# Turning the attention probabilities in halves of 64 queries, with the two heads' score tiles joined

## The chip, the core and the metric
The kernel runs on one core of one Trainium2 chip. The metric is the device time of one execution in microseconds; three runs of the kernel before gave 2627.28, 2629.58 and 2632.4 us, a median of 2629.58.

## The reference
A decoder block on a sequence of 2048 positions of width 1024: modulation from a condition vector, a token mixer, and a feed-forward part with a depthwise convolution. The token mixer has two groups of heads, gated linear attention (4 heads, called GLA here) and 8 softmax heads of width 64. Each softmax head runs three causal dilated windows, (window, dilation) = (128, 1), (512, 4) and (2048, 16), and merges them by their softmax denominators. Cut to the part that the change touches:

```python
def dilated_branch(q, k, v, slopes, window, dilation):
    ...
    s = jnp.einsum('bdhnqe,bdhnke->bdhnqk', qb, kw).astype(jnp.float32) * (E ** -0.5)
    ...
    s = jnp.where(valid, s + alibi, -jnp.inf)
    m = jnp.max(s, axis=-1, keepdims=True)
    p = jnp.exp(s - m)
    den = jnp.sum(p, axis=-1, keepdims=True)
    o = jnp.einsum('bdhnqk,bdhnke->bdhnqe', p, vw.astype(jnp.float32)) / den
    lse = (m + jnp.log(den))[..., 0]
    ...

def dilated_attention_group(q, k, v):
    ...
    weights = jax.nn.softmax(jnp.stack(lses, axis=0), axis=0)
    return jnp.einsum('gbsh,gbshe->bshe', weights, jnp.stack(outs, axis=0))
```

All of it is float32.

## The kernel before
The sequence is worked through in four chunks of 512 positions. For each chunk there are the input projection (`proj`), the mixing (`mix`: two halves of `gla`, then four calls of `attn`, one for each pair of heads), the output projection (`outproj`) and the feed-forward part (`ffn`). The large matrix products split each float32 operand into two parts and issue three matmuls for each product (L292, L293, L294 in `mm3`, 512 columns each, into PSUM banks called `psg`). `beside` (and `along`) writes the mixing of chunk c interleaved with the large products of the chunk before and after, so that TensorE always has large matmuls to issue between the small ones of the mixing. In the end the order on each engine is made by the framework's scheduler, which is switched on with the tile context (`schedule_with_timeline_sim`), from the written order, the dependences and its own estimate of durations. Each engine then executes its list in order.

A call of `attn` for a pair of heads holds, for the three windows, the tiles `s16` (128 queries by 4 blocks of nk = 32(c+1) keys, one tile for each head), `s4` and `sn` (128 queries by 4 blocks of 256 keys, one tile for each head, from the pool entry `big`). `scores` computes the products for the two heads, one on the upper 64 rows of the array and one on the lower 64 (L759; L795 for s16), VectorE adds the bias (L765), ScalarE takes the exponential (L769), VectorE scales by the merge factors (L844 for s4, L855 for sn). L824 and L848 are small products that carry these factors between layouts. Then the probabilities have to stand with keys on the partitions. `turn` (L774) does that for a head at a time: four turns by TensorE (L779) of 128 queries by up to 128 keys into one bank called `psa` (four such banks exist), and one copy back over the same tile, by ScalarE (L171) or VectorE (L173) in alternation. s16 needs one such round, s4 and sn two each (z = P and z = 0; one in chunk 0 for s4). L876 and L881 multiply the turned tiles by the values, L896 turns the result back.

Other places that the change touches: in `gla`, `la` (log decays) takes a buffer of the entry `s16`, and `gv` and `rg` (values and gates) two buffers of `big`; at the start `th` (L308) and the loads of the modulation weights (`wada`, L1017) use `big`. `big` has four buffers of 1024 columns, `s16` two of 512. L617 are the small products of `gla`. Loads and stores named here are issued by SyncE; the weights of the large products (L220) by GpSimd.

## Time and profile before
| | |
|---|---|
| Median of three runs | 2629.58 us |
| Profiled execution | 2630.91 us, its span 2629.1 us |
| TensorE (PE) busy | 2575.6 us, 98% |
| VectorE (DVE) busy | 1923.6 us, 73% |
| ScalarE (ACT) busy | 1278.6 us, 49% |
| GpSimd (POOL) busy | 242.9 us, 9% |
| DMA | 405.10 MB, mean 154 GB/s |

A row of a timeline gives the start, the length, the engine, the line, the operation, the tiles written and read, the shapes and how many instructions were merged into it. The matmuls overlap in time: each is shown from its start until its result is out, so what one takes of TensorE is the distance between the ends of two that follow each other. A matmul of float32 operands shows as two instructions, one of the split operands or a turn as one. "128*128" is the shape of the weights in the array (rows by columns), the second shape that of the operand that streams through it.

### The profile page before, as it was taken

To read this page: it belongs to the slowest core of one execution; us is meant where nothing else is said; L and a number is where in the kernel's file an instruction comes from. 1 tells how busy PE (TensorE), PEld (TensorE's weight loads), DVE (VectorE), ACT (ScalarE), POOL (GpSimd) and SP (SyncE) were. 2 spreads that over 40 slices of the span, in tenths; PEclk is the share of its full clock that TensorE was granted. 3 is DMA by queue.
4 is the path that set the end of the run, shared out by engine and by line. 5 is a ranking of instruction groups with operands and counts; after the bars stand their busy time and mean duration, and the time that the engine had idled before them with its cause. 6 is when DMAs were issued, how large, how long until landed. Compare 5 with 4: busy or idle time off the path is not lost.

```text
span 2629.1 us, 46905 instructions
## 1 busy us (share of the span) xinstructions
PE 2575.6 (98%) x18152; PEld 2112.5 (80%) x18152; DVE 1923.6 (73%) x4124; ACT 1278.6 (49%) x2619; POOL 242.9 (9%) x460
## 2 busy tenths in 40 slices
PE   5999999999999999999999999999999999999999
PEld 3888888788788888888788888877888888788887
DVE  7578877757778777776887777678777775666665
ACT  4556556646555444553545444445455443433332
POOL 0111111101000000000000000000000000000100
PEclk8999999999999999999999999999999999999999
DMA  8766574755633443346434444643344435332222
GB/s 292 255 212 237 195 242 164 232 162 185 210 127 99 130 131 122 117 137 208 141 98 131 140 135 131 235 141 104 122 141 138 136 118 185 128 104 96 97 96 88
DMA packets 192640, 405.10 MB, mean 154 GB/s; under 512 B 19985, under 2 KB 70946, under 8 KB 191138
## 3 DMA queue, kind: packets, MB, share of 16 engines
q0 software_dynamic: 60992, 220.49, 25.6%
q1 hardware_dynamic: 131426, 181.62, 20.8%
q8 instruction: 143, 2.34, 0.4%
q14 instruction: 79, 0.65, 0.1%
HBM read 339.12 MB, written 62.91 MB: 153 GB/s over the span
## 4 chain that ended last, share of the span: by engine, by line
PE 90%; DMA 4%; DVE 3%; issue 1%; ACT 1%; SPq 1%; POOL 0%; DVEq 0%; ACTq 0%
PE psg L292 26%; PE psg L294 25%; PE psg L293 25%; PE psa L759 3%; PE psa L779 2%; PE psa L881 2%; PE psa L617 1%; PE psa L795 1%; DMA x<-x 1%; DMA wada<-in_w_ada_dram 1%; PE psa L876 1%; DVE wlo L227 1%; PE psa L687 1%; PE psa L688 1%; DMA sq<-y 1%
## 5 line engine op out<-in xcount | busy, mean ns | idle before, releaser
L292 PE MATMUL psg<-hhi,whi 128*128 128x512 f32 x1992 | 786.7, 397 | 12.0 <-ACT hhi L428 5.7
L293 PE MATMUL psg<-hlo,whi 128*128 128x512 f32 x1992 | 783.5, 393 | 2.6 <-DVE hlo L430 2.6
L294 PE MATMUL psg<-hhi,wlo 128*128 128x512 f32 x1992 | 782.7, 393 | 0.8 <-DVE wlo L227 0.8
L226 ACT CAST whi<-wraw 128x1024 fp32r<-128x1024 f32 (+1 forms) x391 | 410.4, 1050 | 508.0 <-PE psg L293 404.0
L227 DVE TENSOR_TENSOR wlo<-wraw,whi 128x1024 fp32r<-128x1024 f32 (+1 forms) x391 | 478.0, 1223 | 175.7 <-ACT whi L226 169.9
L292 PEld LDWEIGHTS psg<-hhi,whi 128*128 128x128 f32 x1992 | 375.8, 189 | 99.3 <-ACT hhi L428 8.0
L293 PEld LDWEIGHTS psg<-hlo,whi 128*128 128x128 f32 x1992 | 376.1, 189 | 81.8 <-DVE hlo L430 3.6
L294 PEld LDWEIGHTS psg<-hhi,wlo 128*128 128x128 f32 x1992 | 375.9, 189 | 81.1 <-issue 1.5
L292 PE MATMUL psg<-ghi,whi 128*128 128x512 f32 x744 | 294.2, 398 | 2.7 <-ACT ghi L923 2.5
L294 PE MATMUL psg<-ghi,wlo 128*128 128x512 f32 x744 | 292.8, 394 | 1.6 <-DVE wlo L227 1.6
L293 PE MATMUL psg<-glo,whi 128*128 128x512 f32 x744 | 293.4, 394 | 0.5 <-DVE glo L924 0.5
L998 DVE SCALAR_TENSOR_TENSOR x<-psg,mod,x 128x512 f32<-128x512 f32 x192 | 143.0, 748 | 129.8 <-PE psg L294 127.8
L220 POOL DMA_DIRECT2D wraw<-in_w_up_dram x176 | 93.3, 530 | 1075.6 <-DVE wlo L227 949.0
L292 PE MATMUL psg<-whi,hhi 128*128 128x512 f32 (+2 forms) x512 | 174.1, 345 | 2.6 <-ACT stg L514 1.1
L294 PE MATMUL psg<-whi,hlo 128*128 128x512 f32 (+2 forms) x512 | 174.1, 343 | 0.0
L293 PE MATMUL psg<-wlo,hhi 128*128 128x512 f32 (+2 forms) x512 | 173.5, 340 | 0.0
L292 PEld LDWEIGHTS psg<-ghi,whi 128*128 128x128 f32 x744 | 139.4, 188 | 37.0 <-issue 5.2
L294 PEld LDWEIGHTS psg<-ghi,wlo 128*128 128x128 f32 x744 | 140.3, 189 | 32.2 <-DVE wlo L227 2.0
L293 PEld LDWEIGHTS psg<-glo,whi 128*128 128x128 f32 x744 | 140.3, 189 | 29.5 <-issue 1.4
L769 ACT ACTIVATE big<-big,nm 128x256 f32<-128x256 f32 (+1 forms) x256 | 122.4, 480 | 34.9 <-DVE nm L784 34.7
L953 ACT ACTIVATE y<-psg,conv_b_sb,conv_w_sb 128x512 f32<-128x512 f32 x176 | 136.2, 776 | 3.4 <-PE psg L294 2.0
L954 DVE SCALAR_TENSOR_TENSOR y<-psg,conv_w_sb,y 128x511 f32<-128x511 f32 x176 | 130.7, 743 | 1.4 <-ACT y L953 1.3
(222 smaller groups left out, 3417.7 us busy)
## 6 DMA issues: line engine op xcount, KB each, us to landing
wraw<-in_w_up_dram POOLq DMA_DIRECT2D x176, 512.0 KB, 3.6
wraw<-in_w_down_dram POOLq DMA_DIRECT2D x88, 512.0 KB, 3.6
wraw<-in_w_ch_dram POOLq DMA_DIRECT2D x44, 512.0 KB, 4.2
v<-v SPq DMA_DIRECT2D x68, 256.0 KB, 5.5
wada<-in_w_ada_dram POOLq DMA_DIRECT2D x64, 256.0 KB, 4.8
wraw<-in_w_tokw_dram POOLq DMA_DIRECT2D x32, 512.0 KB, 4.1
wraw<-in_w_out_dram POOLq DMA_DIRECT2D x32, 512.0 KB, 4.4
sq<-in_xT_dram SPq DMA_DIRECT2D x48, 256.0 KB, 3.8
```

Source lines behind the costliest of these rows:

```text
L220: (nc.gpsimd if self.planned else nc.sync).dma_start(raw[:, :n], src)
L226: nc.scalar.copy(hi[:, :n], raw[:, :n])
L227: nc.vector.tensor_tensor(lo[:, :n], raw[:, :n], hi[:, :n].bitcast(F32), op=ALU.subtract)
L292: nc.tensor.matmul(ps, wh, hh, start=first and k == 0, stop=False, skip_group_check=shared)
L293: nc.tensor.matmul(ps, wh, hl, start=False, stop=False, skip_group_check=shared)
L294: self.lastmm = nc.tensor.matmul(ps, wl, hh, start=False, stop=k == n - 1, skip_group_check=shared)
L759: nc.tensor.matmul(at(i, hh, z), q[H[hh], i * P:(i + 1) * P], key(H[hh], i, z), start=True, stop=True, skip_group_check=True)
L769: nc.scalar.activation(t[:, lo:hi], t[:, lo:hi], AF.Exp, bias=nm[:, hh, g, i:i + 1], scale=2.0 ** -(h + 1), accum_out=dn[:, hh, g, i:i + 1])
L779: nc.tensor.transpose(ps[:n, i * P:(i + 1) * P], part(S[hh], i), self.C("id"))
L953: nc.scalar.activation(y, ps, AF.Identity, bias=self.cb[:, b:b + 1], scale=self.cw[:, 2, b:b + 1])
L954: nc.vector.scalar_tensor_tensor(y[:, 1:], ps[:, :T - 1], self.cw[:, 1, b:b + 1], y[:, 1:], op0=ALU.mult, op1=ALU.add)
L998: nc.vector.scalar_tensor_tensor(x1, ps, self.mod[:, 40 + cb:41 + cb], x1, op0=ALU.mult, op1=ALU.add)
```

## The change
`turn` now takes both heads at once. The tiles of a window are one tile for the two heads: `s16` [128, 2, 512], `s4` and `sn` [128, 2, 4, 256]. A round turns, for each block i and head, first the queries 0 to 63 (rows 0 to 63 of the array) into one bank and then the queries 64 to 127 (rows 64 to 127) into a second bank; each of these turns streams 64 columns where one streamed 128 before. One copy for each bank brings back the 64 queries of both heads. In chunk 0 the turns of sn leave out the same block as before. The pool entries follow: `big` has two buffers of 2048 columns, `s16` one of 1024; `gv` and `rg` are halves of one buffer, `th` takes `s16`, and `la` the first half of `s16`, of which there is now one.

```diff
-        th = self.at.tile([P, 1024], F32, name="big", bufs=4)
+        th = self.at.tile([P, 1024], F32, name="s16", bufs=1)
...
-        la = t2("s16", 2)
+        la = self.at.tile([P, 1024], F32, name="s16", bufs=1)[:, 0:T]
...
-        gv, rg = big(), big()
+        big = self.at.tile([P, 2048], F32, name="big", bufs=2)
+        gv, rg = big[:, 0:1024], big[:, 1024:2048]
...
-        s16 = [self.at.tile([P, T], F32, name="s16", bufs=2) for _ in range(2)]
+        s16 = self.at.tile([P, 2, T], F32, name="s16", bufs=1)
+        s16b = s16[:, :, 0:4 * nk].rearrange("p h (i n) -> p h i n", i=4)
...
         def turn(n, b0, part, to):
 
-            for hh in range(2):
-                ps = self.pa()
-                for i in range(b0, 4):
-                    nc.tensor.transpose(ps[:n, i * P:(i + 1) * P], part(S[hh], i), self.C("id"))
-                self.copy(to(S[hh]), ps[:n, b0 * P:].rearrange("p (r n) -> p r n", n=P))
+
+            ps = [self.pa(), self.pa()]
+            for i in range(b0, 4):
+                for hh in range(2):
+                    for m in range(2):
+                        B = slice(64 * m, 64 * m + 64)
+                        nc.tensor.transpose(ps[m][:n, (4 * hh + i) * 64:(4 * hh + i + 1) * 64], part[B, hh, i], self.C("id")[B, B])
+            for m in range(2):
+                self.copy(to[:n, :, b0:, 64 * m:64 * m + 64], ps[m][:n].rearrange("p (h i q) -> p h i q", h=2, i=4)[:, :, b0:])
...
-        s4 = [self.at.tile([P, 4, 256], F32, name="big", bufs=4) for _ in range(2)]
-        sn = [self.at.tile([P, 4, 256], F32, name="big", bufs=4) for _ in range(2)]
+        s4 = self.at.tile([P, 2, 4, 256], F32, name="big", bufs=2)
+        sn = self.at.tile([P, 2, 4, 256], F32, name="big", bufs=2)
...
-        turn(nk, 0, lambda t, i: t[0][:, i * nk:(i + 1) * nk], lambda t: t[0][:nk].rearrange("p (r n) -> p r n", n=P))
+        turn(nk, 0, s16b, s16.rearrange("p h (i q) -> p h i q", i=4))
...
-            turn(P, 0, lambda t, i: t[1][:, i, z:z + P], lambda t: t[1][:, :, z:z + P])
+            turn(P, 0, s4[:, :, :, z:z + P], s4[:, :, :, z:z + P])
...
-            b0 = 0 if (c or z) else 1
-            turn(P, b0, lambda t, i: t[2][:, i, z:z + P], lambda t: t[2][:, b0:, z:z + P])
+            turn(P, 0 if (c or z) else 1, sn[:, :, :, z:z + P], sn[:, :, :, z:z + P])
...
+        bigs = [self.at.tile([P, 2048], F32, name="wada", tag="big", bufs=2) for _ in range(2)]
         for k in range(KD):
-            big = [self.at.tile([P, 1024], F32, name="wada", tag="big", bufs=4)]
+            big = [bigs[k % 4 // 2][:, k % 2 * 1024:k % 2 * 1024 + 1024]]
```

All other reads and writes of these tiles are rewritten for the new shapes (`outs[hh][...]` becomes `outs[:, hh, ...]`, and so on). In the changed file the turns are line L783, L824 is L828, L848 is L852, L876 is L879.

The scheduler makes another order from this. TensorE, second chunk, second pair of heads: the beginning of the turns of s4 (`big`), behind the small product of the merge factors. Before:

```order
L848 MATMUL psa<-xm,consts_sb 128x32
L779 MATMUL psa<-consts_sb,big 128x128 x12
L292 MATMUL psg<-ghi,whi 128x512
L293 MATMUL psg<-glo,whi 128x512
L294 MATMUL psg<-ghi,wlo 128x512
```

Now, at the same place:

```order
L852 MATMUL psa<-xm,consts_sb 128x32
L783 MATMUL psa<-consts_sb,big 128x64 x3
L292 MATMUL psg<-ghi,whi 128x512
L783 MATMUL psa<-consts_sb,big 128x64 x29
L293 MATMUL psg<-glo,whi 128x512
L294 MATMUL psg<-ghi,wlo 128x512
```

The 16 turns of s4 stood as 12 and, ten large matmuls later, 4; the 32 half turns stand as 3 and 29 with one large matmul between. The turns of sn that follow in the same call, on TensorE, before:

```order
L293 MATMUL psg<-glo,whi 128x512
L779 MATMUL psa<-consts_sb,big 128x128 x5
L294 MATMUL psg<-ghi,wlo 128x512
L779 MATMUL psa<-consts_sb,big 128x128 x3
L292 MATMUL psg<-ghi,whi 128x512
L293 MATMUL psg<-glo,whi 128x512
L779 MATMUL psa<-consts_sb,big 128x128 x4
L294 MATMUL psg<-ghi,wlo 128x512
```

And now:

```order
L294 MATMUL psg<-ghi,wlo 128x512
L292 MATMUL psg<-ghi,whi 128x512
L783 MATMUL psa<-consts_sb,big 128x64 x32
L293 MATMUL psg<-glo,whi 128x512
L294 MATMUL psg<-ghi,wlo 128x512
```

These 16 turns stood in four runs (4, 5, 3, 4); the 32 halves stand in one, 18 large matmuls behind the run of 29. The end of the turns of s4 on TensorE in the same call (the run of 29 above), now, with the numbers of the banks; psa_10903 and psa_10904 are the banks of the first round, psa_10923 and psa_10924 those of the second, in each pair first the bank of queries 0 to 63:

```order
L783 MATMUL psa_10903<-consts_sb_452,big_10575 128x64
L783 MATMUL psa_10904<-consts_sb_452,big_10575 128x64
L783 MATMUL psa_10923<-consts_sb_452,big_10575 128x64 x4
L783 MATMUL psa_10924<-consts_sb_452,big_10575 128x64 x5
L783 MATMUL psa_10923<-consts_sb_452,big_10575 128x64
L783 MATMUL psa_10924<-consts_sb_452,big_10575 128x64
```

The two halves mostly alternate, but where a bank came free late in the scheduler's reckoning, several halves of one bank stand together. Over the whole program the 600 turns stood in 99 unbroken runs, the 1200 halves stand in 98.

## Rows read from the trace of the kernel before

**Rows 1.** The page: busy time, share and instructions of TensorE; the chain of waits that ended last, by engine and by line.

```profile
PE 2575.6 (98%) x18152; PEld 2112.5 (80%) x18152; DVE 1923.6 (73%) x4124; ACT 1278.6 (49%) x2619; POOL 242.9 (9%) x460
...
PE 90%; DMA 4%; DVE 3%; issue 1%; ACT 1%; SPq 1%; POOL 0%; DVEq 0%; ACTq 0%
PE psg L292 26%; PE psg L294 25%; PE psg L293 25%; PE psa L759 3%; PE psa L779 2%; PE psa L881 2%; PE psa L617 1%; PE psa L795 1%; DMA x<-x 1%; DMA wada<-in_w_ada_dram 1%; PE psa L876 1%; DVE wlo L227 1%; PE psa L687 1%; PE psa L688 1%; DMA sq<-y 1%
```

**Rows 2.** Busy time by stretch of the span: from and to, length, then PE, PEld, DVE, ACT and POOL busy with their instructions, the granted clock of TensorE, the DMA share and GB/s.

```profile
0.00:160.00 160.00, 129.77 (x617) 106.33 (x618) 112.05 (x206) 77.81 (x115) 20.06 (x41) 0.96 0.75 261
160.00:2300.00 2140.00, 2120.53 (x16103) 1737.13 (x16102) 1603.10 (x3597) 1090.12 (x2370) 193.28 (x365) 1.00 0.48 155
```

**Rows 3.** What TensorE waited for, longest first in total: the waiting line, what released it, us in total, times, longest.

```profile
PE psa L406 <- DVE rstd L400: 14.7, 1, 14.7
PE psg L292 <- ACT hhi L428: 5.7, 2, 4.2
...
PE psa L795 <- DMA qf<-q: 4.4, 2, 2.5
```

**Rows 4.** The turns, line L779, by tile: instructions, duration min/median/max in ns, first and last start, forms.

```profile
L779 PE MATMUL psa<-consts_sb,big x472: 270/272/328, 450.9 to 2173.7; 128*128 128x128 f32 x158
...
L779 PE MATMUL psa<-consts_sb,s x128: 271/273/278, 438.1 to 2150.1; 128*32 128x128 f32 x32, 128*64 128x128 f32 x32, 128*96 128x128 f32 x32, 128*128 128x128 f32 x32
```

**Rows 5.** Timeline of TensorE (start, length) around a run of 16 turns, its first turn alone once more, and around a run of 8 turns with a weight of 32 columns.

```profile
1101.20 0.39 PE L294 MATMUL psg<-hhi,wlo 128*128 128x512 f32 x1
1101.43 0.27 PE L779 MATMUL psa<-consts_sb,big 128*128 128x128 f32 x1
...
1101.43 1.91 PE L779 MATMUL psa<-consts_sb,big 128*128 128x128 f32 x16
1103.10 0.48 PE L292 MATMUL psg<-hhi,whi 128*128 128x512 f32 x1
1103.41 0.40 PE L293 MATMUL psg<-hlo,whi 128*128 128x512 f32 x1
...
509.83 0.33 PE L824 MATMUL psa<-xm,consts_sb 128*128 128x64 f32 x2
510.00 1.04 PE L779 MATMUL psa<-consts_sb,s 128*32 128x128 f32 x8
510.79 0.48 PE L294 MATMUL psg<-whi,hlo 128*128 128x512 f32 x1
```

**Rows 6.** Timeline of TensorE around eight instructions of the scores in chunk 0 (64 rows by 128 columns of weights, 128 columns moving; upper and lower rows of the array in turn), the first alone and all.

```profile
407.44 0.39 PE L292 MATMUL psg<-hhi,whi 128*128 128x512 f32 x1
407.75 0.37 PE L759 MATMUL psa<-kw,qf 64*128 64x128 f32 x1
...
407.75 0.72 PE L759 MATMUL psa<-kw,qf 64*128 64x128 f32 x8
408.40 0.50 PE L293 MATMUL psg<-hlo,whi 128*128 128x512 f32 x1
```

**Rows 7.** Timeline of TensorE around sixteen instructions of L617 with weights of 64 by 64 and 64 columns moving (eight on the upper rows, then eight on the lower): the first alone, all, four near the end, the last alone, and the large matmuls around them.

```profile
760.72 0.39 PE L294 MATMUL psg<-whi,hlo 128*128 128x512 f32 x1
761.04 0.27 PE L617 MATMUL psa<-pt 64*64 64x64 f32 x1
...
761.04 0.96 PE L617 MATMUL psa<-pt 64*64 64x64 f32 x16
...
761.61 0.39 PE L617 MATMUL psa<-pt 64*64 64x64 f32 x4
...
761.78 0.22 PE L617 MATMUL psa<-pt 64*64 64x64 f32 x1
761.93 0.50 PE L292 MATMUL psg<-hhi,whi 128*128 128x512 f32 x1
762.27 0.39 PE L293 MATMUL psg<-hlo,whi 128*128 128x512 f32 x1
```

**Rows 8.** Weight loads by form (line, engine PEld, tiles, rows*columns of the weights, count, then busy us and mean ns of one, idle before).

```profile
L617 PEld LDWEIGHTS psa<-pt 64*32 64x32 f32 x2816 | 30.8, 107 | 21.9 <-issue 10.2 <-PE psg L293 5.3 <-ACT rstd L408 2.4
L759 PEld LDWEIGHTS psa<-kw,qf 64*128 64x128 f32 x256 | 25.4, 190 | 10.4 <-issue 5.6 <-ACT s L769 1.1 <-ACT halo L960 0.7
...
L779 PEld LDWEIGHTS psa<-consts_sb,s 128*128 128x128 f32 x32 | 3.6, 147 | 0.0
...
L779 PEld LDWEIGHTS psa<-consts_sb,s 128*64 128x64 f32 x32 | 3.5, 119 | 0.0
L779 PEld LDWEIGHTS psa<-consts_sb,s 128*32 128x32 f32 x32 | 3.1, 104 | 0.4
```

**Rows 9.** Groups by form on VectorE and ScalarE: the copies back and the scaling of sn (count, busy us, mean ns of one, idle before and its releaser).

```profile
L173 DVE COPY big<-psa 128x512 f32<-128x512 f32 x56 | 38.3, 684 | 5.1 <-PE psa L779 4.7
L855 DVE TENSOR_SCALAR big<-big,f 128x256 f32<-128x256 f32 x120 | 33.3, 348 | 0.3
...
L171 ACT COPY big<-psa 128x512 f32<-128x512 f32 x56 | 32.7, 587 | 67.2 <-PE psa L779 67.1
```

**Rows 10.** Timeline of one call (second chunk): VectorE's scaling of s4, and the run of turns that reads it.

```profile
1088.16 2.18 DVE L844 TENSOR_SCALAR big<-big,f 128x256 f32<-128x256 f32 x8
...
1092.97 1.51 PE L779 MATMUL psa<-consts_sb,big 128*128 128x128 f32 x12
```

More of the change, by code (lines that the diff above doesn't have):

```diff
@@ L584, in gla @@
         t2 = lambda name, bufs=1: self.at.tile([P, T], F32, name=name, tag=name, bufs=bufs)
-        big = lambda: self.at.tile([P, 1024], F32, name="big", bufs=4)
         tk = slice(a * 256, a * 256 + 256)
@@ L796, in attn @@
             for r4 in range(4):
-                TTR(s16[hh][:, r4 * nk:(r4 + 1) * nk], ps[:, r4 * nk:(r4 + 1) * nk], self.C("b16")[:, P - nk:P], mx[:, hh, 0, r4:r4 + 1])
+                TTR(s16b[:, hh, r4], ps[:, r4 * nk:(r4 + 1) * nk], self.C("b16")[:, P - nk:P], mx[:, hh, 0, r4:r4 + 1])
         v16 = self.at.tile([P, 16, P], F32, name="v16", tag="kt", bufs=2)
@@ L806, in attn @@
         scores(qf, lambda R, r, z: k4[R, r].rearrange("p w m -> p (w m)")[:, z:], z4, self.C("b4"), s4, 1)
-        exps(0, lambda hh, i: (s16[hh], hh, 0, i, i * nk, (i + 1) * nk))
+        exps(0, lambda hh, i: (s16b[:, hh, i], hh, 0, i, 0, nk))
         yield
         scores(qn, lambda R, b, z: k1[R, b * P + z:b * P + 256], z1, self.C("b1"), sn, 2)
-        exps(1, lambda hh, i: (s4[hh][:, i], hh, 1, i, z4(i), 256))
-        S = [(s16[hh], s4[hh], sn[hh]) for hh in range(2)]
+        exps(1, lambda hh, i: (s4[:, hh, i], hh, 1, i, z4(i), 256))
         v4 = self.at.tile([P, 2, 4, P], F32, name="v4", bufs=1)
@@ L815, in attn @@
         yield
-        exps(2, lambda hh, i: (sn[hh][:, i], hh, 2, i, z1(i), 256))
+        exps(2, lambda hh, i: (sn[:, hh, i], hh, 2, i, z1(i), 256))
         mv = md.rearrange("p q h g r -> p (q h) g r")[:, :, 2]
@@ L875, in attn @@
                 for j in range(4):
-                    nc.tensor.matmul(O16[32 * j:32 * j + 32, cols(r4, hh)], S[hh][0][:nk, r4 * P + 32 * j:r4 * P + 32 * j + 32], v16[:nk, 4 * j + r4, H[hh]], start=True, stop=True, skip_group_check=True)
+                    nc.tensor.matmul(O16[32 * j:32 * j + 32, cols(r4, hh)], s16[:nk, hh, r4 * P + 32 * j:r4 * P + 32 * j + 32], v16[:nk, 4 * j + r4, H[hh]], start=True, stop=True, skip_group_check=True)
         O = self.pa()
@@ L886, in attn @@
                 for hh in range(2):
[L887 removed]
+                    add(hh, sg(O[H[hh]], r4), v4[:, z // P, r4, H[hh]], s4[:, hh, r4, z:z + P])
         for z in (P, 0):
@@ L890, in attn @@
                 for hh in range(2):
-                    add(hh, s1(O[H[hh]], b), v1[:, b + z // P, H[hh]], S[hh][2][:, b, z:z + P])
+                    add(hh, s1(O[H[hh]], b), v1[:, b + z // P, H[hh]], sn[:, hh, b, z:z + P])
         acc = weigh(O16, 0)
```

7 lines of the change are left out of this document (3 added, 4 removed).

## The prediction
> **What bounds the kernel now.** I read the page first, then the busy time by stage, then TensorE's waits, then single runs on TensorE. The page says that TensorE is busy 98% of the span and holds 90% of the chain that ended last; the line of the turns, L779, is 2% of it [rows 1]. By stage the idle time is mostly at the start: 30.2 of the first 160 us, and 19.5 of the next 2140, where the attention lies [rows 2]. TensorE's waits name what it waited for, 14.7 us of start-up and then small things of other steps; no row among them is a turn's [rows 3]. The granted clock is 1.00, the 2.4 GHz level, in that second stretch [rows 2]. So the time there is the sum of what each instruction takes on TensorE, and an edit there counts in full; VectorE and ScalarE are busy 75% and 51% of it and count only if TensorE begins to wait for them.
>
> **What a turn costs now.** The view of the line counts 472 turns of `big` and 128 of `s` [rows 4]: 600. A run of 16 begins with one that ends at 1101.43+0.27 = 1101.70, 0.11 after the matmul before it (1101.20+0.39 = 1101.59); the run ends at 1103.34, so each takes 1.64/15 = 0.109 us. The two matmuls behind it end 0.24 and 0.23 later, which is what a 512-column matmul always takes here: going into a run and out of it costs nothing, and for the narrow weight of 32 columns neither (eight end 0.88 after the matmuls before them, the next large one 0.23 later) [rows 5]. So 600 × 0.109 = 65.4 us.
>
> **What the new turns cost.** The trace has no turn of 64 rows, so the price is built from its neighbours.
> Overlap of the two halves: the scores (L759) hold a 64x128 weight for each half of the rows. In chunk 0, with 128 columns moving, eight of them end 0.64 us after the matmul before; the first ends after 0.29, which leaves 0.35 for three pairs, 0.11 to 0.12 a pair: two loads and two streams in the time of one [rows 6].
> Time of one half: L617's 64x64 matmuls stream 64 columns. Four of them in a row span 0.39 us, the last takes 0.22 of that, so they follow each other every 0.058 [rows 7]. That is the lower bound of a pair; the upper one is two in turn, 0.116.
> Load: weight loads of matmuls take 107 ns for 32 columns and 190 for 128, so 28 per 32 columns. Those of turns take 104, 119 and 147 for 32, 64 and 128: 14 to 15 per 32, so 128 columns load in about 0.058 [rows 8]. Load and stream of a half are then equal, and a pair should keep to 0.058. The Trainium skill ("TensorE: Matmul & The Clock Gate", LDWEIGHTS) has a rule against this change: a load's time goes by its columns, not its rows, so halving the rows doubles the loading; by it 128 columns take 107 ns, and the sum would go by twice my price of a pair. The matmuls' rows agree with it, the turns' rows do not; what it would do here is the rival of slow loads.
>
> **How many.** 1200 halves. In the changed order 430 times a half is followed at once by the other half; 340 stand alone, mostly as eight of one bank and then eight of the other, since the scheduler lets a half go when its own bank is free. That is 770 steps × 0.058 = 44.7 us. Blocks overlap a little: L617's run is eight of one row half and eight of the other and takes 0.69/0.058 = 12 steps after the first, 13 in all for 16 [rows 7]. Some twenty such blocks save about two steps each beyond the one that I already counted as a pair: 2.0 us. I take 42.7; the bounds are 600 and 1200 steps, 34.8 and 69.6. So the turning itself saves 65.4 - 42.7 = 22.7 us.
>
> **What it adds: going in and out.** A run that uses part of the rows is not free to enter. Before L617's run the last matmul ends at 761.11; the run's first ends at 761.31, 0.20 later instead of 0.058. Behind it the next matmul ends 0.43 after the run (762.43 against 762.00) and the one after that 0.23 later [rows 7]. The scores show the same 0.43 on the way out [rows 6]. So a run costs 0.14 + 0.20 = 0.34 us, as array and weight loads empty and fill again. The changed order has 98 runs of turns (99 before, free), 95 of which end at a full-size matmul; three end at L879, which pays on entry either way: 98 × 0.14 + 95 × 0.20 = 32.7 us. The other runs on part of the array fall from 180 to 176, which gives 4 × 0.3 = 1.2 back. The Trainium skill ("TensorEngine Tiling (Array Packing)", Theoretical Speedup) promises up to twice the speed where a dimension is 64 or less, which alone would take 32.7 off; the same page (Tiling Modes, Key Properties) says that a change of mode drains the engine. The trace agrees with the second: 0.34 us each time.
>
> **The rest at nothing, and what hides it.** There are still two copies per turn of 512 columns, 0.59 us on ScalarE and 0.68 on VectorE [rows 9]; they lie beside TensorE's large matmuls, now for two banks at once. The scaling that a turn of `s4` needs, eight of VectorE, ended at 1090.34, and TensorE came to the turn at 1092.97: 2.6 us of cover [rows 10]. Needing both heads' tiles at once asks for four more of these, 1.1 us, which fits. The joined tiles (`big` two of 2048, `s16` one) ask for the release of both halves, which were released together anyway. The load of the second half's `la` now waits for L600 of the first half, the first matmuls of that half, with loads of x and stores of k and rg behind it on SyncE's queue; a whole half of mixing lies before its own use. At the start `th` leaves `big`; the first 160 us could move by a microsecond either way. If the cover goes, it is the rival of waits.
>
> **Sum.** -22.7 + 32.7 - 1.2 = +8.8 us. The profiled execution took 2630.9 (its span 2629.1 and 1.8 around it), so 2639.7; it lies 1.3 above the median of the three runs, 2629.6, so the forecast is 2638.4. Own range 2633 to 2644: half a microsecond for each hundredth in the step, and some microseconds for a reshuffled order.
>
> **Rivals.**
> No price at the border (not slower). Turns with a weight of 32 columns enter today without delay [rows 5], where matmuls with a part of the array pay, so the array may not count a turn as a change of form while the halves still overlap. Then only the saving is left: -22.7 - 1.2 = -23.9, 2605.7. It decides from 0.24 us a run downwards (23.9/98). Against it: matmuls of 64 rows pay 0.34 everywhere. Chance 0.10.
> Neither overlap nor price: the halves go one by one as ordinary turns. 1200 × 0.058 - 65.4 - 1.2 = +3.0, 2632.6. For it: no turn in the trace uses part of the rows. Chance 0.10.
> Price without overlap: +4.2 + 32.7 - 1.2 = +35.7, 2665. Against it: the pairs of rows 6. Chance 0.08.
> Slow loads: a pair takes 0.11, as those pairs do with their 190 ns loads. Some 5/6 of the steps (those with 128 columns) cost 0.05 more, about 620 × 0.053 = +33 on top, 2671. Chance 0.05.
> Waits take the place: a turn of `sn` needs two banks at once out of four, and before it lie 18 large matmuls (4.1 us), in which VectorE has eight scalings of 0.35 and two copies of 0.68 [rows 9], 4.2 us, besides the feed-forward's steps. If TensorE waits 0.5 to 1 us in each of 16 calls, it is 8 to 16 us more: 2646 to 2654. For it: VectorE is 75% busy; against it, no such wait stands in the trace [rows 3]. Chance 0.15.
>
> **The numbers.** The forecast has 0.50 (0.02 left for anything else), the five rivals 0.10, 0.10, 0.08, 0.05 and 0.15. From 2612 to 2666 the forecast, waits, lone halves and price without overlap are held; slow loads and most of the free border are out. About 0.2% (5.3 us) can be told from no change here: faster is the free border and what a luckier order could do, 0.17; within it are lone halves without price and the low end of the forecast, 0.20; slower 0.63.
>
> **What will show it.** Two turns start together and pairs follow each other every 0.058 us; the first of a run ends 0.20 after the matmul before it; the large matmul behind a run ends 0.43 after it; the turns' line falls from about 65 to 56 us on TensorE while the large matmuls' lines gain 17 to 19. TensorE's idle time stays near 53 us; if it grows by over 5, waits were the cause. A large matmul that ends 0.23 after a run, or pairs at 0.11, would make me wrong.

## The result, and the profile after

The changed kernel takes 2640.91 us, median of five runs (2637.25 to 2643.66); the kernel before, run beside it on the same chip, 2627.28 us (2624.75 to 2632.4). The ratio is 1.0050, with a 95% interval of 1.0037 to 1.0062: 13.1 us slower, 9.7 to 16.3. The forecast was 2638.4 as a time, and 8.8 us as a difference. The time is met within 2.5 us; the difference is 4 us larger than the forecast, and part of why the time agrees so well is luck: the median of before, on which the forecast stood, fell from 2629.6 to 2627.3 with more runs.

The two profiled executions differ by 6.3 us alone (2637.25 against 2630.91): after's lies at the low end of its five, before's above its median. A stretch of lower clock in the profiled execution of before, shown below under the pools, is a part of what is missing (5.0 us); a sum from a single profile carries differences of this size, so the experiments are judged by medians.

The page, TensorE's and the other engines' busy time:

```profile
PE 2583.3 (98%) x18752; PEld 2100.3 (80%) x18752; DVE 1924.8 (73%) x4124; ACT 1279.3 (49%) x2620; POOL 242.6 (9%) x460
```

600 more instructions on TensorE, and 7.7 us more busy than in [rows 1]. The span is 2635.5, so TensorE idles for 52.2 us (53.5 before). VectorE and ScalarE do as much as before. By stretch, with the columns of [rows 2]:

```profile
0.00:160.00 160.00, 130.19 (x620) 107.16 (x621) 111.81 (x207) 78.61 (x116) 20.05 (x41) 0.96 0.77 263
160.00:2300.00 2140.00, 2121.48 (x16671) 1718.90 (x16671) 1598.07 (x3586) 1086.16 (x2365) 192.14 (x362) 1.00 0.48 154
```

The start is as before, the middle is still a busy TensorE at the 2.4 GHz level. What is new must be in what TensorE does. Its waits, in the form of [rows 3]:

```profile
PE psa L406 <- DVE rstd L400: 14.4, 1, 14.4
...
PE psa L461 <- ACT sqr L455: 1.6, 1, 1.6
PE psa L783 <- DVE xm L854: 1.5, 2, 1.0
```

The half turns (L783) wait twice, 1.5 us in all. The other new row, L461 behind `sqr`, belongs to a step that the change does not touch; it comes back below. The line of the turns by tile, in the form of [rows 4]:

```profile
L783 PE MATMUL psa<-consts_sb,big x944: 221/223/274, 455.7 to 2177.3; 64*128 64x64 f32 x189
L783 PE MATMUL psa<-consts_sb,s x256: 216/216/273, 440.1 to 2156.0; 64*32 64x64 f32 x32, 64*64 64x64 f32 x32, 64*96 64x64 f32 x32, 64*128 64x64 f32 x32
```

1200 halves. A length here includes the time in TensorE's pipeline; what one costs is the distance between ends, and for that the timeline is read. An undisturbed run of 32 halves of `big`: the matmul before it, the first half alone, the first pair, the whole run and the two large matmuls behind it. Then a run of eight that stand alone: its first, all, and the next two. Then sixteen halves of `s` with weights of 64 columns: the first pair, all, and the next two.

```profile
1095.88 0.39 PE L294 MATMUL psg<-hhi,wlo 128*128 128x512 f32 x1
1096.20 0.27 PE L783 MATMUL psa<-consts_sb,big 64*128 64x64 f32 x1
...
1096.20 0.28 PE L783 MATMUL psa<-consts_sb,big 64*128 64x64 f32 x2
...
1096.20 1.21 PE L783 MATMUL psa<-consts_sb,big 64*128 64x64 f32 x32
1097.34 0.50 PE L292 MATMUL psg<-hhi,whi 128*128 128x512 f32 x1
1097.67 0.39 PE L293 MATMUL psg<-hlo,whi 128*128 128x512 f32 x1
...
1089.44 0.27 PE L783 MATMUL psa<-consts_sb,big 64*128 64x64 f32 x1
...
1089.44 0.71 PE L783 MATMUL psa<-consts_sb,big 64*128 64x64 f32 x8
1090.08 0.50 PE L293 MATMUL psg<-hlo,whi 128*128 128x512 f32 x1
1090.42 0.39 PE L294 MATMUL psg<-hhi,wlo 128*128 128x512 f32 x1
...
1076.40 0.25 PE L783 MATMUL psa<-consts_sb,s 64*64 64x64 f32 x2
...
1076.40 0.64 PE L783 MATMUL psa<-consts_sb,s 64*64 64x64 f32 x16
1076.97 0.50 PE L292 MATMUL psg<-hhi,whi 128*128 128x512 f32 x1
1077.31 0.39 PE L293 MATMUL psg<-hlo,whi 128*128 128x512 f32 x1
```

The matmul before the first run ends at 1096.27, the first half at 1096.47, 0.20 later. The two of a pair end within 0.01 of each other. The run ends at 1097.41: 15 more pairs in 0.94, 0.0625 a pair. The large matmul behind it ends at 1097.84, 0.43 later, the next 0.22 after that. So a run pays at both ends just as L617's did in [rows 7]. The eight alone take 1090.15 - 1089.71 = 0.44 for seven steps, again 0.0625: a half by itself costs as much as a pair. With 64 columns of weights seven pairs take 1077.04 - 1076.65 = 0.39, 0.056 a pair.

To see what this does to the whole program I gave each instruction of TensorE the time from the end of the one before it (or from its own start, if that is later) to its own end, and added these up by kind, from the starts and lengths in each trace. "Large" are L292, L293 and L294, "scores" the line L759 of before, "idle" the span less TensorE's busy time; the other small products, 240 to 241 us in each, make up the rest of the span.

```
us                       turns   large   scores   idle
before                    66.6  2199.1     69.7   53.5
joined tiles, whole turns 66.2  2197.7     68.2   55.9
changed                   59.6  2215.5     67.9   52.2
four tiles, half turns    56.0  2209.2     68.8   51.4
four tiles, held          46.5  2207.1     73.8   50.3
changed, held             46.6  2204.8     67.0   52.0
halves by half of rows    66.7  2213.9     67.5   54.4
```

From before to the changed kernel the turns fall by 7.0 and the large matmuls, not one of which was altered, rise by 16.4. The price behind a run accounts for it: 92 runs end at a large matmul that takes 0.425 on average instead of 0.231, which is 17.8 us. Against the joined tiles the rise is 17.8 too. What the turns save goes, more than twice over, into the first matmul behind each run.

### The profile page after: what moved, and what is told of

Its sections match the earlier page's. It is cut to its first block, busy times and chain, and to the rows that moved or that the text cites. A ratio compares the mean times of both kernels' runs of the same rounds, so it can differ in the third digit from the quotient of the medians.

```text
span 2635.5 us, 48115 instructions
## 1 busy us (share of the span) xinstructions
PE 2583.3 (98%) x18752; PEld 2100.3 (80%) x18752; DVE 1924.8 (73%) x4124; ACT 1279.3 (49%) x2620; POOL 242.6 (9%) x460
## 4 chain that ended last, share of the span: by engine, by line
PE 67%; DVE 3%; DMA 2%; ACT 1%; issue 1%; SPq 0%; DVEq 0%; ACTq 0%
PE psg L292 20%; PE psg L293 19%; PE psg L294 19%; PE psa L760 2%; PE psa L783 2%; PE psa L884 2%; PE psa L617 1%; DMA x<-x 1%; DVE wlo L227 1%; DMA v<-v 1%; PE psa L800 1%; PE psa L879 0%; PE psa L688 0%; PE psa L687 0%; DMA sq<-y 0%
## 5 line engine op out<-in xcount | busy, mean ns | idle before, releaser
L292 PE MATMUL psg<-hhi,whi 128*128 128x512 f32 x1992 | 788.9, 398 | 13.0 <-ACT hhi L428 5.7
L293 PE MATMUL psg<-hlo,whi 128*128 128x512 f32 x1992 | 784.7, 394 | 2.4 <-DVE hlo L430 2.4
L294 PE MATMUL psg<-hhi,wlo 128*128 128x512 f32 x1992 | 783.0, 393 | 0.3 <-DVE wlo L227 0.3
L292 PEld LDWEIGHTS psg<-hhi,whi 128*128 128x128 f32 x1992 | 376.2, 189 | 101.4 <-ACT hhi L428 7.7
L293 PEld LDWEIGHTS psg<-hlo,whi 128*128 128x128 f32 x1992 | 376.3, 189 | 82.8 <-DVE hlo L430 3.5
L294 PEld LDWEIGHTS psg<-hhi,wlo 128*128 128x128 f32 x1992 | 376.3, 189 | 81.8 <-issue 1.5
L292 PE MATMUL psg<-ghi,whi 128*128 128x512 f32 x744 | 295.6, 399 | 0.7 <-ACT ghi L926 0.4
L294 PE MATMUL psg<-ghi,wlo 128*128 128x512 f32 x744 | 292.5, 393 | 1.0 <-DVE wlo L227 1.0
L293 PE MATMUL psg<-glo,whi 128*128 128x512 f32 x744 | 292.8, 394 | 0.7 <-DVE glo L927 0.7
L292 PE MATMUL psg<-whi,hhi 128*128 128x512 f32 (+2 forms) x512 | 172.6, 342 | 1.9 <-ACT stg L514 0.8
L293 PE MATMUL psg<-wlo,hhi 128*128 128x512 f32 (+2 forms) x512 | 173.4, 339 | 0.0
L294 PE MATMUL psg<-whi,hlo 128*128 128x512 f32 (+2 forms) x512 | 173.0, 340 | 0.0
L292 PEld LDWEIGHTS psg<-ghi,whi 128*128 128x128 f32 x744 | 139.8, 188 | 36.0 <-issue 6.7
L294 PEld LDWEIGHTS psg<-ghi,wlo 128*128 128x128 f32 x744 | 140.1, 188 | 32.3 <-DVE wlo L227 1.4
L293 PEld LDWEIGHTS psg<-glo,whi 128*128 128x128 f32 x744 | 140.1, 188 | 30.4 <-issue 1.2
L958 DVE SCALAR_TENSOR_TENSOR y<-psg,conv_w_sb,y 128x510 f32<-128x510 f32 x176 | 131.2, 746 | 0.8
```

What stands on the lines that cost most here:

```text
L292: nc.tensor.matmul(ps, wh, hh, start=first and k == 0, stop=False, skip_group_check=shared)
L293: nc.tensor.matmul(ps, wh, hl, start=False, stop=False, skip_group_check=shared)
L294: self.lastmm = nc.tensor.matmul(ps, wl, hh, start=False, stop=k == n - 1, skip_group_check=shared)
L958: nc.vector.scalar_tensor_tensor(y[:, 2:], ps[:, :T - 2], self.cw[:, 0, b:b + 1], y[:, 2:], op0=ALU.mult, op1=ALU.add)
```

## The experiments

All ten kernels were timed in five rounds against the kernel before on the same chip; differences are worked out from the ratio, as a share of before's median there, with its interval in brackets.

**Joined tiles, whole turns.** The tiles and pools of the change, with the turns as before:

```diff
-            ps = [self.pa(), self.pa()]
...
+            for hh in range(2):
+                ps = self.pa()
+                for i in range(b0, 4):
+                    nc.tensor.transpose(ps[:n, i * P:(i + 1) * P], part[:, hh, i], self.C("id"))
+                self.copy(to[:n, hh, b0:], ps[:n, b0 * P:].rearrange("p (r n) -> p r n", n=P))
```

> Joined tiles and the new pool entries of the change, but a head at a time in whole turns of 128 queries, a bank for each head, as before. Theory of borders (the loss comes from runs that use half of the rows: about 0.155 us more on entry and 0.195 behind it, against 0.05 saved for each pair): no run uses half of the rows, so it is as fast as the kernel before, within 4 us of it. Theory of tiles (the loss comes from buffers that come free together and from the order that this makes): as slow as the changed kernel, about 13 us over the kernel before.

Measured 2630.52 us beside 2624.20, ratio 1.0021: 5.5 us slower [3.1 to 7.6]. The tiles and pools, which the forecast put at nothing, cost about 5 us with no half turn in the program. That is a good third of the result; two kernels further down take one pool each.

**Held half turns.** The changed kernel, but the first half turn of each round of `s4` and of `sn` waits for the last scaling of that round, where before it waited only for the tile columns that it reads. This keeps a round from being started early and broken off:

```diff
-        def turn(n, b0, part, to):
+        def turn(n, b0, part, to, held=None):
...
-                        nc.tensor.transpose(ps[m][:n, (4 * hh + i) * 64:(4 * hh + i + 1) * 64], part[B, hh, i], self.C("id")[B, B])
+                t = nc.tensor.transpose(ps[m][:n, (4 * hh + i) * 64:(4 * hh + i + 1) * 64], part[B, hh, i], self.C("id")[B, B])
+                if held is not None:
+                    self.tc.add_manual_dep(t.ins, held.ins.name, SY)
+                    held = None
...
-            turn(P, 0, s4[:, :, :, z:z + P], s4[:, :, :, z:z + P])
+            turn(P, 0, s4[:, :, :, z:z + P], s4[:, :, :, z:z + P], h4)
```

> The changed kernel, with the first half turn of each round of s4 and sn held until the last scaling of that tile is done. In its order the 1200 halves stand in 52 runs instead of 98, in 648 steps instead of 770. Theory of borders, with the prices of the changed kernel's trace: 648 x 0.061 + 52 x (0.155 + 0.195) = 57.7 us against 66.6 + 0.4 for the whole turns of the kernel before, so about 9 us faster than the kernel before and 20 or more faster than the changed one; a run there that costs nothing at its border would make this run equal to the changed kernel. Theory of tiles: as slow as the changed kernel. Theory of waits (both heads and two banks needed at once): slower than the changed kernel, since it waits for more.

Measured 2616.85 us beside 2624.20, ratio 0.9971: 7.6 us faster than before [4.5 to 10.5], and so some 21 faster than the changed kernel. The same 1200 halves now stand in 52 runs and 648 steps instead of 98 and 770. By the rows above, 46 runs at 0.14 + 0.20 are 15.6 us and 122 steps at 0.0625 are 7.6: 23 us. An added wait made the kernel faster, and the number of runs is what decides. The page's busy time of this kernel, 24.9 us less on TensorE than in the changed one with as many instructions:

```profile
PE 2558.4 (98%) x18752; PEld 2087.9 (80%) x18752; DVE 1922.0 (74%) x4124; ACT 1277.4 (49%) x2620; POOL 242.4 (9%) x460
```

**Chained half turns.** The changed kernel, with each half turn of a round ordered behind the one before it in the program (an order only, no wait), so that the two halves of a turn stay neighbours:

```diff
+                if prev[0] is not None:
+                    self.tc.add_manual_dep(t.ins, prev[0].ins.name, NS)
+                prev[0] = t
...
+            prev[0] = None
```

> The changed kernel, with the half turns of a round kept in their written order on TensorE, so that a half is followed by the other half: 626 steps instead of 770 in 95 runs instead of 98. Theory of borders: 144 x 0.061 + 3 x 0.35 = 9.8 us less than the changed kernel, still 2 to 6 us over the kernel before. If lone halves overlapped anyway, it would be equal to the changed kernel but for 1 us.

Measured 2632.97 us beside 2624.20, ratio 1.0028: 7.3 us slower than before [4.2 to 10.2], 6 less than the changed kernel's 13.1. The order has 95 runs and 626 steps: three runs fewer and 144 steps fewer. The turns' time falls from 59.6 to 51.8. So pairing up the lone halves brings steps, and the runs' price stays. The 2 to 6 us over before that were expected lie partly inside the interval, the value above them: the turns bring 7.8 of the 9.8 us that were counted, and a stretch that lies before the first turn, shown below under the pools, is 2.4 us longer here than in the changed kernel.

**Halves by half of the rows.** The changed kernel with all halves of the upper rows of a round ahead of all of the lower, kept in that order as in the chained kernel:

```diff
-            for i in range(b0, 4):
-                for hh in range(2):
-                    for m in range(2):
+            todo = [(i, hh, m) for m in range(2) for i in range(b0, 4) for hh in range(2)]
+            for i, hh, m in todo:
```

> The changed kernel with all halves of queries 0 to 63 of a round ahead of all halves of 64 to 127, in that order on TensorE: nearly no pairs, 1102 steps in 80 runs. Theory of borders with overlap only between neighbours: 1102 x 0.062 + 80 x 0.35 = 96 us against 67 for the whole turns before, about 29 us slower than the kernel before. If blocks of eight and eight overlapped too, it would be within 5 us of the changed kernel.

Measured 2643.93 us beside 2624.20, ratio 1.0075: 19.7 us slower [16.3 to 23.1]. It is slower than the changed kernel, as it must be if neighbours overlap, but less so than a count of its 1102 steps says. TensorE's timeline of one run of 31 halves there:

```profile
1032.32 0.39 PE L294 MATMUL psg<-ghi,wlo 128*128 128x512 f32 x1
1032.63 1.57 PE L787 MATMUL psa<-consts_sb,big 64*128 64x64 f32 x31
1034.13 0.50 PE L292 MATMUL psg<-ghi,whi 128*128 128x512 f32 x1
1034.46 0.39 PE L293 MATMUL psg<-glo,whi 128*128 128x512 f32 x1
```

From the large matmul's end (1032.71) to the run's (1034.20) are 1.49 us. After the 0.20 of the first half 1.29 are left for 30 more, which one by one would take 1.88. The ends in the trace show why: in part of the run they come in twos, 0.06 apart, ten times in all. Over the whole program 271 halves end within 0.02 us of the one before, where 1102 steps leave only 98 that stand next to a half of the other rows. So halves overlap with others that are not their neighbours in the order; which ones, the trace does not tell. That overlap, which the prediction took as two steps a block, is larger: about a third of this run's steps.

**Which pool.** Two kernels with whole turns take one pool each from the change. The small one: `s16`, `la` and `th` in one tile of 1024 columns.

```diff
-        th = self.at.tile([P, 1024], F32, name="big", bufs=4)
+        th = self.at.tile([P, 1024], F32, name="s16", bufs=1)
...
-        la = t2("s16", 2)
+        la = self.at.tile([P, 1024], F32, name="s16", bufs=1)[:, 0:T]
...
-        s16 = [self.at.tile([P, T], F32, name="s16", bufs=2) for _ in range(2)]
+        s16w = self.at.tile([P, 2, T], F32, name="s16", bufs=1)
+        s16 = [s16w[:, 0], s16w[:, 1]]
```

> The kernel before with only the small pool changed as in the change: one tile of 1024 columns under the name s16 (one buffer) for both heads' 16-branch scores, and the gated branch's la and the start's tanh out of the same buffer; the score tiles called big stay four separate ones, and the turns stay whole. TensorE's order has 99 runs and no price differs in it. Joined tiles with whole turns took 5.6 us more than before. Theory 'small pool' (the second half's la must wait until the first half's la, or a round's scores, are done with, and the loads queued behind it on SyncE come late, in the stretch from 160 to 310 us): this kernel takes those 5 to 6 us, 2630 beside a before of 2624.5. Theory 'large pool': it takes nothing, within 1.5 us of before. Theory 'chance of the order' (neither pool alone moves it): within 2 us for this kernel and for the large pool alone.

Measured 2626.53 us beside 2624.63, ratio 1.0007: 1.8 us [-0.8 to 4.7], not told from nothing.

The large one: `big` as two tiles of 2048 columns.

```diff
-        gv, rg = big(), big()
+        big = self.at.tile([P, 2048], F32, name="big", bufs=2)
+        gv, rg = big[:, 0:1024], big[:, 1024:2048]
...
-        s4 = [self.at.tile([P, 4, 256], F32, name="big", bufs=4) for _ in range(2)]
+        s4w = self.at.tile([P, 2, 4, 256], F32, name="big", bufs=2)
+        s4 = [s4w[:, 0], s4w[:, 1]]
```

> The kernel before with only the large pool changed as in the change: big is two buffers of 2048 columns instead of four of 1024, for the score tiles, for the gated branch's gv and rg and for the loads at the start; the small pool and the whole turns are as before. Theory 'large pool' (a pair of tiles comes free only when the later of the two does): 5 to 6 us more than before, 2630 beside 2624.5, with TensorE idle for longer at 160 to 310 us. Theory 'small pool': within 1.5 us of before. Theory 'chance of the order': within 2 us.

Measured 2629.51 us beside 2624.63, ratio 1.0020: 5.2 us slower [2.1 to 8.7], nearly all of the joined tiles' 5.5. By the medians it is more likely the large pool, though the two intervals overlap. Its trace shows a place. TensorE's timeline there, the idle time and its releaser in brackets:

```profile
248.56 0.39 PE L292 MATMUL psg<-hhi,whi 128*128 128x512 f32 x1
252.41 0.79 PE L461 MATMUL psa<-sqr,blk 128*128 128x512 f32 x1 [3.46 <-ACT sqr L455]
253.13 0.33 PE L617 MATMUL psa<-pt 64*32 64x32 f32 x8
253.59 0.79 PE L462 MATMUL psa<-sqr,blk 128*128 128x512 f32 x1
```

and the busy time by stretch around it:

```profile
248.00:252.00 4.00, 0.95 (x5) 0.45 (x3) 3.32 (x6) 3.96 (x8) 0.00 (x0) 1.00 0.07 29
252.00:256.00 4.00, 3.46 (x68) 2.30 (x69) 3.93 (x7) 3.33 (x6) 0.53 (x1) 0.54 0.42 149
256.00:260.00 4.00, 4.00 (x12) 3.10 (x12) 4.00 (x8) 1.51 (x3) 0.53 (x1) 0.61 0.68 235
```

The same matmul in before, which did not wait:

```profile
244.56 0.39 PE L461 MATMUL psa<-sqr,blk 128*128 128x512 f32 x1
```

Two prices stand here. TensorE waits 3.46 us for ScalarE's `sqr` at L461, a matmul of a norm's statistics; in before, large matmuls run on through this time. ScalarE does not stand still while TensorE waits (busy 3.96 of the 4 us from 248), it is behind with its list. And behind the wait the granted clock is 0.54 and 0.61, the 1.2 GHz level for most of 8 us: the same 128x512 matmul takes 0.79 instead of 0.39. That costs (1 - 0.54) × 4 + (1 - 0.61) × 4 = 3.4 us once more. The joined tiles' trace has the same wait at the same place, 3.5 us, and 0.50 and 0.80 in the same two stretches. The stretch as a whole, first in before, then in the joined tiles:

```profile
160.00:310.00 150.00, 148.86 (x1232) 124.80 (x1231) 121.82 (x230) 92.22 (x170) 20.86 (x40) 1.00 0.63 213
```

```profile
160.00:310.00 150.00, 143.64 (x1201) 119.97 (x1200) 115.57 (x219) 88.89 (x164) 21.13 (x40) 0.98 0.62 207
```

TensorE idles here for 1.1 us in before, 6.4 with the joined tiles, 5.3 with the large pool alone (3.46 at L461 and 1.2 at L566, which waits for ScalarE too) and 2.2 with the small pool alone. In the changed kernel it is 3.4 (its wait at L461 is 1.6 us; the clock stays at 1.00 behind it, but is at 0.57 from 233 to 237 us), in the ones derived from it 2.5 to 5.2. What the wait takes varies, then, and so does whether the clock falls.

Both prices and what else lies there can be had in one number, and before any turn runs (the first starts at 438.1 us in before, at 440.1 in the changed kernel): the time from the eighth start of L461 (at 172 to 174 us) to the sixteenth.

```
us from the eighth to the sixteenth L461
big as four of 1024   before 147.2, four tiles with half turns 147.6, the same held 147.3,
                      small pool alone 148.2
big as two of 2048    changed, held 150.2; joined tiles held 151.2; changed 151.3;
                      held with la elsewhere 152.2; chained 153.7; large pool alone 154.2;
                      halves by half of rows 154.6; joined tiles 154.7
```

All eight kernels with the large pool of two lie 3.0 to 7.5 us above before, the three with four tiles at most 1.0. So the large pool is the cause, with no half turn at work, and the changed kernel's own profile has 4.1 us of it. Further back the traces point at a load of x that ScalarE waits for. The same instruction in before, and then with the large pool alone:

```profile
215.78 0.63 ACT L395 ACTIVATE sq<-sq 128x512 f32<-128x512 f32 x1 [2.32 <-DMA sq<-in_xT_dram]
```

```profile
218.83 0.63 ACT L395 ACTIVATE sq<-sq 128x512 f32<-128x512 f32 x1 [5.62 <-DMA sq<-in_xT_dram]
```

That the lag begins with this load was not tested.

The profiled execution of before has the same pair of prices at another place. Its longest wait from 460 to 620 us, and the busy time of two stretches behind it that overlap:

```profile
PE psa L795 <- DMA qf<-q: 1.9, 1, 1.9
```

```profile
558.00:568.00 10.00, 10.00 (x41) 7.91 (x42) 3.19 (x25) 6.08 (x34) 0.00 (x0) 0.50 0.08 26
560.00:580.00 20.00, 20.00 (x95) 16.06 (x95) 10.02 (x37) 12.78 (x46) 1.63 (x4) 0.79 0.22 67
```

1.9 us of waiting for a transfer (to 556.3 us), and then ten us at the 1.2 GHz level, 5.0 us more. A longer wait at the same line in the same profile had no such price:

```profile
623.60 0.76 PE L795 MATMUL psa<-kt,qf 64*32 64x32 f32 x64 [2.51 <-DMA qf<-q]
```

```profile
623.00:640.00 17.00, 16.40 (x155) 12.69 (x156) 11.91 (x64) 11.28 (x44) 1.07 (x2) 1.00 0.68 210
```

So the length of a wait alone does not tell whether the clock falls.

**Whole turns, held.** The joined tiles with whole turns and the wait of the held half turns:

```diff
-                    nc.tensor.transpose(ps[:n, i * P:(i + 1) * P], part[:, hh, i], self.C("id"))
+                    t = nc.tensor.transpose(ps[:n, i * P:(i + 1) * P], part[:, hh, i], self.C("id"))
+                    if held is not None:
+                        self.tc.add_manual_dep(t.ins, held.ins.name, SY)
+                        held = None
```

> The joined tiles with whole 128-query turns, a head at a time, and the first turn of each round of the 4- and the near branch made to wait for the round's last scaling, as in the kernel with held half turns that took 7.5 us less than before. Runs of turns on TensorE fall from 101 to 74. Theory 'a border costs, and only half turns have a dear one': a whole turn's run costs little at its two ends, so this gains about 2 us on the joined tiles alone, 2628 to 2629 beside a before of 2624.5. Rival 'holding itself helps' (the scalings, evictions or large matmuls gain by the later, denser round whatever the turns' shape): about 12 us less than the joined tiles alone, 2618.

Measured 2627.18 us beside 2624.63, ratio 1.0014: 3.7 us slower than before [0.3 to 6.8], about 2 less than the joined tiles without the wait, which within the two intervals may also be nothing. Runs fall from 101 to 74; 2 us would be some 0.07 us each. So holding by itself brings little or nothing: runs of whole turns are nearly free, and only runs of halves are worth joining.

**Held half turns, `la` elsewhere.**

```diff
-        la = self.at.tile([P, 1024], F32, name="s16", bufs=1)[:, 0:T]
+        la = self.at.tile([P, T], F32, name="la", tag="pt", bufs=5)
```

> The kernel with held half turns, with la taken from the pool of small tiles that has five buffers (pt) instead of sharing the one s16 buffer. Theory 'small pool': the 5 to 6 us that the joined tiles cost come back, less 2 us for TensorE's own order, which has a few more part-array borders here: 2613, and less idle of TensorE at 160 to 310 us. Theory 'large pool' or 'chance of the order': 2617 to 2620, no less than the held half turns alone (2616.9).

Measured 2616.35 us beside 2624.63, ratio 0.9965: 9.2 us faster than before [5.5 to 12.9], where the held half turns had 7.6 [4.5 to 10.5]. The two can't be told apart, and TensorE idles longer from 160 to 310 us here (4.5 us) than there (2.5). But the edit did more than free `la` from the shared buffer. Its trace has a new wait for the load of `la`, and behind it the lower clock:

```profile
675.97 2.05 PE L600 MATMUL psa<-consts_sb,la 128*128 128x128 f32 x8 [3.32 <-DMA la<-la]
```

```profile
676.00:680.00 4.00, 4.00 (x75) 3.43 (x75) 1.94 (x4) 0.00 (x0) 0.00 (x0) 0.50 1.06 390
```

The held half turns have no such wait. So this run does not settle what the shared buffer costs `la`; the small pool alone, at 1.8 us [-0.8 to 4.7], is the better bound.

**Half turns with four tiles.** If the large pool costs 5 us, half turns without it must cost the rest. The tiles and pools are those of before, and a bank goes back in two copies:

```diff
+                        nc.tensor.transpose(ps[m][:n, (4 * hh + i) * 64:(4 * hh + i + 1) * 64], part(S[hh], i)[B], self.C("id")[B, B])
+            for m in range(2):
+                for hh in range(2):
+                    self.copy(to(S[hh])[:, :, 64 * m:64 * m + 64], ps[m][:n, (4 * hh + b0) * 64:(4 * hh + 4) * 64].rearrange("p (r n) -> p r n", n=64))
```

> The kernel before with the half turns of the change alone: the four score tiles, the two s16 buffers and the pools stay as before, and a half turn's bank goes back to the tiles in two copies (one for each head) where the change has one for both, so copies double and are half as long. 89 runs of turns, 727 steps. Counted as in the prediction, with each step at 0.058 us, each run at its two borders and the other part-array borders of this order, TensorE needs 4.8 us more than before; the same count gives 7.8 us for the change. Theory 'turns and pool apart' (the change's 13.6 us are some 8 of turns and some 5 of the large pool's wait at 160 to 310 us): this kernel takes 4 to 6 us more than before, 2629 beside 2624.5, and TensorE stands still at 160 to 310 us no longer than in before (1.1 us). Rival 'dearer borders' (the pool adds nothing on top of half turns, and the whole 13.6 us are theirs): 13.6 x 4.8 / 7.8, 8.4 us more, 2633, or above that if the doubled copies come late.

Measured 2633.76 us beside 2626.51, ratio 1.0026: 6.8 us slower [4.2 to 9.7]. The value lies between the two expectations and its interval holds both, so by itself it is unclear. The place does speak: from 160 to 310 us TensorE idles for 1.5 us (1.1 in before), and the clock is at 1.00.

```profile
160.00:310.00 150.00, 148.54 (x1231) 124.51 (x1230) 121.48 (x229) 93.59 (x172) 21.26 (x40) 1.00 0.63 215
```

With the others it closes a table of two by two: whole turns and four tiles 0, joined tiles alone 5.5, half turns alone 6.8 (with the doubled copies in it), both 13.1. The sum of the two is 12.3, so they add up within their intervals.

**Half turns with four tiles, held.** The same with the held wait:

```diff
-        def turn(n, b0, part, to):
+        def turn(n, b0, part, to, held=None):
...
+                        if held is not None:
+                            self.tc.add_manual_dep(t.ins, held.ins.name, SY)
+                            held = None
```

> The same four tiles and two copies for a bank, with the first half turn of each round of the 4- and the near branch waiting for the round's last scaling. 54 runs of turns, 638 steps; by the count of the prediction TensorE needs 3.6 us less than before (13.7 less for the held half turns on the joined tiles, whose order has fewer other part-array borders). Theory 'turns and pool apart': 3.6 us less than before with nothing added by the pools, 2621, so no better than the held half turns on joined tiles (2616.9). Rival 'dearer borders': with 54 runs instead of 98 it gains at least as much as the held half turns on joined tiles did, 7.5 us or more, 2617 or below. A result above 2625 would say that the doubled copies are waited for.

Measured 2624.11 us beside 2626.51, ratio 0.9996: 1.1 us faster [-2.4 to 4.5]. The count's 3.6 lies inside, the rival's 7.5 and more does not. Against the kernel with half turns and four tiles it gains 8 us. That it stays behind the held half turns on joined tiles is not the turns' doing: both spend 46.5 us on them, but the scores take 73.8 us here and 67.0 there in the table above. Their order was laid out otherwise: the scores stand in 61 unbroken runs here and in 50 there, and these runs pay at their ends too. The count puts 10.1 us between the two held kernels (13.7 - 3.6) and 6.5 were measured; the 3.6 us by which the kernel with the large pool falls short are about that pool's price in its profile (150.2 against 147.3 in the table under the pools).

## Why the prediction was right, and where it was not

**The price at the border: right.** It was taken from L617 [rows 7] as 0.14 going in and 0.20 coming out. The first half of a run ends 0.20 after the matmul before it, the large matmul behind a run ends 0.425 after it (mean of 92), and the held kernel, with 46 runs fewer, shows by an experiment what the timeline alone suggests. The first rival, a free border, is out; so is price without overlap, since the two of a pair end together, and with both the rival that had neither.

**The pair: a little dear.** The forecast was 0.058 for each step; it is 0.0625 where the weight has 128 columns and 0.056 for the narrower ones. The turns' line came to 59.6 us without its waits, where "from about 65 to 56" stood. Five sixths of the 770 steps, some 640, have 128 columns; at 0.0045 more each they are 2.9 us, nearly the whole difference. The loads by form, as in [rows 8]:

```profile
L783 PEld LDWEIGHTS psa<-consts_sb,big 64*128 64x128 f32 x944 | 44.0, 138 | 22.3 <-issue 10.3 <-DVE xm L854 2.8 <-DVE big L173 1.6
...
L783 PEld LDWEIGHTS psa<-consts_sb,s 64*32 64x32 f32 x64 | 2.3, 93 | 0.9 <-issue 0.6
L783 PEld LDWEIGHTS psa<-consts_sb,s 64*96 64x96 f32 x64 | 2.0, 123 | 0.3
L783 PEld LDWEIGHTS psa<-consts_sb,s 64*64 64x64 f32 x64 | 1.9, 108 | 0.3
```

From 93 to 138 they rise by 15 for each 32 columns, on 64 rows as on 128, which is 0.060 for 128 columns. The stream of 64 columns is the same for all of them, and only the steps with 128 columns are longer than 0.056, which points to the load as what sets the pace there. The Trainium skill ("TensorE: Matmul & The Clock Gate", LDWEIGHTS) goes by columns too, with 107 ns for 128; in this trace the step is 62.5 ns, so the rule's direction shows here and its figure does not. Slow loads as a rival, with 0.11 a pair, are out.

**The number of steps: right for this order.** Lone halves did take a step each, as counted. That blocks of different rows overlap when they stand behind each other was put at 2.0 us; the experiment with halves by half of the rows shows that it can be far more, since the 19.7 measured there is well below what 1102 steps of the forecast's price come to (332 more steps than the changed kernel at 0.058 are 19.3, on top of its 13.1, less 18 runs at 0.34: 26), and the turns' own time rises from 59.6 to only 66.7.

**The sum of the turns: right.** 8.8 was forecast. The changed kernel stands 7.6 above the joined tiles (13.1 - 5.5), and half turns with four tiles 6.8 above before. So two misses stand against each other, a little too much for the turns and nothing for the pools, and the second is the larger.

**The joined tiles at nothing: wrong.** This is the step that failed: "The joined tiles (`big` two of 2048, `s16` one) ask for the release of both halves, which were released together anyway." For the scores nothing speaks against it: TensorE's waits at L795 were 4.4 us in before, 2.5 with the large pool alone and 3.2 with the joined tiles (L797 there). But the pool also holds the gated branch's `gv` and `rg` and the loads at the start, and with it the order of instructions that have nothing to do with turns came out differently, and between 172 and 330 us TensorE falls behind: 4.1 us in the changed kernel's profile, 7.0 with the large pool alone, in which the wait of 3.46 us at L461 and the 3.4 us of lower clock behind it are the main part. By medians the large pool costs 5.2 us [2.1 to 8.7]. The forecast looked for the price in the first 160 us and at `la`; the first 160 us are unchanged (129.77 and 130.19 us busy), and for `la` nothing shows that can be told from noise.

**Waits of the turns: right.** TensorE waits for half turns twice, 1.5 us together, where the rival had 8 to 16. Idle time in all fell from 53.5 to 52.2 us in the two profiles.

What stays open: through which of its users (scores, gated branch, loads at the start) the large pool brings about the wait at L461 was not tried, and how often the clock falls behind that wait in runs without a profile is not known. The mean granted clock of all runs is 0.9948 with the large pool alone and 0.9960 in before beside it, and 0.0012 of 2628 us are some 3 us; but with half turns and four tiles it is lower than in before too (0.9940 and 0.9949), so that part of the difference does not belong to the pool alone.

## What to carry over

Work on part of the array's rows is priced by the run and not by the instruction: here a run of half turns pays 0.34 us at its two ends and earns 0.109 - 0.0625 = 0.047 for each whole turn that it replaces by a pair. So it pays from a little over seven turns on where every half meets its partner, from about eight in the held order (648 steps for 600 turns) and from about twelve in the changed one (770 steps): 98 runs of six turns on average lose, and 52 runs of eleven to twelve win. Where a scheduler breaks such work up, a wait that holds its first instruction until all of it is ready can gain time (2616.85 us, the fastest with its sister at 2616.35). And a change of pools is an edit of its own: time it alone, since everything that shares the pool is laid out anew.

## What the runs showed of the hardware that was not expected

A turn's half on its own costs as much as two at once (0.0625 us), and a half may run beside one of the other rows that is not its neighbour in the order (30 halves in 1.29 us instead of 1.88). A single wait of 3.46 us on TensorE was followed by 8 us at a granted clock of 0.54 and 0.61, so its true price was twice its length; after 1.9 us in before the clock stood at 0.50 for ten us, after 2.5 us in the same profile it stayed at 1.00, and so it did after 1.6 us in the changed kernel.
